# A ReLU-mean over rows: 127 rows a partition and a separate block of 128 rows, in place of 128 rows a partition

## The chip, the cores and the metric

The kernel runs on one core of a Trainium2 chip. The metric is device time in microseconds (us), measured outside the profile. An execution's span on the core is about 1.8 us shorter than its device time.

## The reference

```
x: 32 x 512 x 1024 float32          # 16,384 rows of 1024 values, 67.1 MB
out = mean(maximum(x, 0), axis=-1)  # 16,384 float32, 65.5 KB
```

There are few operations per byte: each value is read once and added once.

## The kernel before

Partition p holds rows 128p to 128p+127, so two neighbouring partitions start 512 KiB apart in memory. Seven tiles of 16 rows a partition are loaded in three rotating buffers. The last 16 rows are loaded in pieces of 8, 4, 2 and 1 rows, and the very last row in three column pieces. Rows go alternately to VectorE and ScalarE (L20 and L15 in the profile). Only SyncE's queue (SP) loads and stores.

```
def dve_row(nc, src, acc, init=None):                      # VectorE, L20
    nc.vector.tensor_scalar(out=src, in0=src, scalar1=0.0, scalar2=init,
        op0=ALU.max, op1=ALU.add, accum_out=acc)
# act_row (ScalarE, L15): activation Relu with accum_out=acc
...
xr = xf.rearrange("(p j) d -> p j d", p=P, j=J)            # J = 128
outr = out.flatten().rearrange("(p j) -> p j", p=P, j=J)
NB = 16; full = J // NB - 1
row_pieces = [8, 4, 2, 1]; col_pieces = [512, 256, 256]
...
for t in range(full):
    j0 = t * NB
    xt = in_pool.tile([P, NB, D], F32, name="xt")          # bufs=3
    nc.sync.dma_start(out=xt, in_=xr[:, j0:j0 + NB, :])
    rows(xt, 0, NB, j0)
...
for n in row_pieces:
    nc.sync.dma_start(out=xt[:, lo:lo + n, :], in_=xr[:, j0 + lo:j0 + lo + n, :])
    lo += n
# the last row's three column pieces are loaded here
...
for n in row_pieces[:-1]:
    rows(xt, lo, n, j0)
    lo += n
act_row(nc, prev[:, :512], part[:, 0:1])                   # row 126, one half each
dve_row(nc, prev[:, 512:], part[:, 1:2])
# row 127: 256 + 256, 128 + 128 columns side by side, then 256 on VectorE
...
nc.vector.scalar_tensor_tensor(out=res[:, J - 1:J], ...)
nc.sync.dma_start(out=outr, in_=res)                       # 512 B a partition
```

Of the kernel before, what the change touches and what calls it, by code (L numbers as in the profile page):

```python
# [1 line left out]

# [4 lines left out]

F32 = mybir.dt.float32
ALU = mybir.AluOpType
ACT = mybir.ActivationFunctionType  # L10


def act_row(nc, src, acc):

    nc.scalar.activation(out=src, in_=src, func=ACT.Relu, accum_out=acc)  # L15


def dve_row(nc, src, acc, init=None):

    nc.vector.tensor_scalar(  # L20
        out=src, in0=src, scalar1=0.0, scalar2=init,
        op0=ALU.max, op1=ALU.add, accum_out=acc,
    )


@with_exitstack
def kernel(
    ctx: ExitStack,
    tc: tile.TileContext,
    x: bass.AP,  # L30
    out: bass.AP,
):
    nc = tc.nc
    P = nc.NUM_PARTITIONS
    xf = x.flatten_outer_dims()
    R, D = xf.shape
    assert R % P == 0
    J = R // P
    inv = 1.0 / D
    xr = xf.rearrange("(p j) d -> p j d", p=P, j=J)  # L40
    outr = out.flatten().rearrange("(p j) -> p j", p=P, j=J)
    xlast = xr[:, J - 1, :]

    NB = 16
    full = J // NB - 1

    row_pieces = [8, 4, 2, 1]
    assert sum(row_pieces) == NB - 1
    col_pieces = [512, 256, 256]
    assert sum(col_pieces) == D  # L50

    in_pool = ctx.enter_context(tc.tile_pool(name="in", bufs=3))
    res_pool = ctx.enter_context(tc.tile_pool(name="res", bufs=1))
    sums = res_pool.tile([P, J], F32)
    res = res_pool.tile([P, J], F32)
    part = res_pool.tile([P, 10], F32)

    def rows(xt, lo, n, j0):

        for k in range(lo, lo + n):  # L60
            j = j0 + k
            (dve_row if j % 2 else act_row)(nc, xt[:, k, :], sums[:, j:j + 1])

    def finish(lo, hi):
        nc.gpsimd.tensor_scalar(  # L65
            out=res[:, lo:hi], in0=sums[:, lo:hi], scalar1=inv, scalar2=0.0, op0=ALU.mult, op1=ALU.add,
        )

    for t in range(full):
        j0 = t * NB  # L70
        xt = in_pool.tile([P, NB, D], F32, name="xt")
        nc.sync.dma_start(out=xt, in_=xr[:, j0:j0 + NB, :])  # L72
        rows(xt, 0, NB, j0)

    j0 = full * NB
    xt = in_pool.tile([P, NB, D], F32, name="xt")
    prev, last = xt[:, NB - 2, :], xt[:, NB - 1, :]
    lo = 0
    for n in row_pieces:
        nc.sync.dma_start(out=xt[:, lo:lo + n, :], in_=xr[:, j0 + lo:j0 + lo + n, :])  # L80
        lo += n
    c = 0
    for w in col_pieces:
        nc.sync.dma_start(out=last[:, c:c + w], in_=xlast[:, c:c + w])
        c += w

    finish(0, j0)
    lo = 0
    for n in row_pieces[:-1]:
        rows(xt, lo, n, j0)  # L90
        lo += n
    finish(j0, j0 + lo)



    act_row(nc, prev[:, :512], part[:, 0:1])
    dve_row(nc, prev[:, 512:], part[:, 1:2])
    nc.gpsimd.tensor_scalar(  # L98
        out=res[:, J - 2:J - 1], in0=part[:, 0:1], scalar1=part[:, 1:2], scalar2=inv, op0=ALU.add, op1=ALU.mult,
    )  # L100
    act_row(nc, last[:, :256], part[:, 2:3])
    dve_row(nc, last[:, 256:512], part[:, 3:4])
    nc.gpsimd.tensor_scalar(  # L103
        out=part[:, 4:5], in0=part[:, 2:3], scalar1=inv, scalar2=0.0, op0=ALU.mult, op1=ALU.add,
    )
    act_row(nc, last[:, 512:640], part[:, 5:6])
    dve_row(nc, last[:, 640:768], part[:, 6:7], init=part[:, 3:4])
    nc.scalar.activation(  # L108
        out=part[:, 7:8], in_=part[:, 5:6], func=ACT.Identity, scale=inv, bias=part[:, 4:5],
    )  # L110
    dve_row(nc, last[:, 768:], part[:, 8:9], init=part[:, 6:7])
    nc.vector.scalar_tensor_tensor(  # L112
        out=res[:, J - 1:J], in0=part[:, 8:9], scalar=inv, in1=part[:, 7:8], op0=ALU.mult, op1=ALU.add,
    )
    nc.sync.dma_start(out=outr, in_=res)


# [1 line left out]
_INS = ['x']  # L119
_OUTS = [((32, 512), 'float32')]  # L120


# [23 lines left out]
```

## Time and profile before

| | before |
|---|---|
| device time, median of 4 | 164.65 us |
| the profiled execution: device time, span | 164.37 us, 162.6 us |
| VectorE, ScalarE busy | 46%, 43% |
| first input packet starts, last one ends | 1.75 us, 158.65 us |
| VectorE's last result, issue of the store | 160.08 us, 160.15 us |

The packet times come from the trace's DMA records: each has a start, a duration and a size. They were put on the profile's axis by the first memset, which is at 0.24 us. I call the stretch from the last input packet's end to the end of VectorE's last result the *tail*: 1.43 us here.

The page of the kernel before gives the bound: the load queue's packets fill 96.2% of the 16 DMA engines' time, and the chain that ended last is made of input transfers.

```profile
DVE 74.8 (46%) x135; ACT 69.6 (43%) x134; POOL 1.2 (1%) x8
...
DMA packets 2162, 67.19 MB, mean 413 GB/s; under 512 B 240, under 2 KB 624, under 8 KB 880
...
q1 hardware_dynamic: 2160, 67.18, 96.2%
...
DMA 84%; DVE 13%; SPq 1%; issue 0%; DVEq 0%
...
out_dram<-res SPq DMA_DIRECT2D x1, 64.0 KB, 1.5
```

VectorE's 13% of the chain needs care: two of its stretches, 9.2 us each, stand between a landing and the next load's issue, and earlier loads keep the DMA engines busy meanwhile (the DMA row has no gap). Only the third stretch, after the stream, adds to the span.

That stretch is in VectorE's timeline. The columns are start, duration (us), engine, line, operation, output and input; an idle time and its releaser follow in brackets where there is one.

```profile
154.03 1.22 DVE L20 TENSOR_SCALAR_CACHE_REDUCE xt<-xt 128x1024 f32<-128x1024 f32 x1
...
155.18 1.22 DVE L20 TENSOR_SCALAR_CACHE_REDUCE xt<-xt 128x1024 f32<-128x1024 f32 x1
156.32 0.08 DVE L20 DVE_READ_ACCUMULATOR xt<-xt 128x1 f32 x1
156.53 1.22 DVE L20 TENSOR_SCALAR_CACHE_REDUCE xt<-xt 128x1024 f32<-128x1024 f32 x1
157.67 0.08 DVE L20 DVE_READ_ACCUMULATOR xt<-xt 128x1 f32 x1
157.83 0.69 DVE L20 TENSOR_SCALAR_CACHE_REDUCE xt<-xt 128x512 f32<-128x512 f32 x1
...
158.47 0.42 DVE L20 TENSOR_SCALAR_CACHE_REDUCE xt<-xt 128x256 f32<-128x256 f32 x1
...
159.92 0.16 DVE L112 SCALAR_TENSOR_TENSOR res<-part 128x1 f32<-128x1 f32 x1
```

VectorE starts the four-row piece at 154.03 and could take a new row at 156.32, before the two-row piece is there (156.53). It then keeps up with the landings: 157.83 is the landing of row 126.

### The profile page before, as it was taken

To read this page: it belongs to the slowest core of one execution; us is meant where nothing else is said; L and a number is where in the kernel's file an instruction comes from. 1 tells how busy PE (TensorE), PEld (TensorE's weight loads), DVE (VectorE), ACT (ScalarE), POOL (GpSimd) and SP (SyncE) were. 2 spreads that over 40 slices of the span, in tenths; PEclk is the share of its full clock that TensorE was granted. 3 is DMA by queue.
4 is the path that set the end of the run, shared out by engine and by line. 5 is a ranking of instruction groups with operands and counts; after the bars stand their busy time and mean duration, and the time that the engine had idled before them with its cause. 6 is when DMAs were issued, how large, how long until landed. Compare 5 with 4: busy or idle time off the path is not lost.

```text
span 162.6 us, 358 instructions
## 1 busy us (share of the span) xinstructions
DVE 74.8 (46%) x135; ACT 69.6 (43%) x134; POOL 1.2 (1%) x8
## 2 busy tenths in 40 slices
DVE  0000039900696008940099201990049800698993
ACT  3000039700694008920099002980049600696882
POOL 0000000000000000000000000000000000000001
DMA  7979989989988997997997998997998997998980
GB/s 258 516 322 451 516 355 419 516 371 403 516 387 387 516 435 339 516 435 339 516 484 326 484 484 355 451 500 339 451 500 355 435 516 306 451 435 379 415 334 17
DMA packets 2162, 67.19 MB, mean 413 GB/s; under 512 B 240, under 2 KB 624, under 8 KB 880
## 3 DMA queue, kind: packets, MB, share of 16 engines
q1 hardware_dynamic: 2160, 67.18, 96.2%
q14 instruction: 2, 0.02, 0.0%
HBM read 67.11 MB, written 0.07 MB: 413 GB/s over the span
## 4 chain that ended last, share of the span: by engine, by line
DMA 84%; DVE 13%; SPq 1%; issue 0%; DVEq 0%
DMA xt<-in_x_dram 84%; DVE xt L20 13%; SPq L80 1%; SPq L72 0%; DVE res L112 0%; DVEq L20 0%; DVEq L112 0%
## 5 line engine op out<-in xcount | busy, mean ns | idle before, releaser
L20 DVE TENSOR_SCALAR_CACHE_REDUCE xt<-xt 128x1024 f32<-128x1024 f32 (+1 forms) x65 | 73.7, 1195 | 85.1 <-DMA xt<-in_x_dram 84.8
L15 ACT ACTIVATE xt<-xt 128x1024 f32<-128x1024 f32 (+1 forms) x66 | 67.0, 1016 | 89.2 <-DMA xt<-in_x_dram 89.2
L15 ACT ACTIVATION_READ_ACCUMULATOR xt<-xt 128x1 f32 x66 | 12.3, 187 | 0.0
L20 DVE DVE_READ_ACCUMULATOR xt<-xt 128x1 f32 x65 | 5.4, 83 | 0.0
L65 POOL TENSOR_SCALAR res<-sums 128x112 f32<-128x112 f32 (+1 forms) x2 | 0.5, 252 | 157.2 <-DVE xt L20 157.2
L15 ACT ACT_TABLE_LOAD x1 | 1.3, 1283 | 0.7 <-PEq L130 0.7
L20 DVE TENSOR_SCALAR_CACHE_REDUCE xt<-xt,part 128x128 f32<-128x128 f32 (+1 forms) x2 | 0.8, 412 | 0.1
L108 ACT ACTIVATE part<-part 128x1 f32<-128x1 f32 x1 | 0.3, 294 | 0.1
L98 POOL TENSOR_SCALAR res<-part 128x1 f32<-128x1 f32 x1 | 0.3, 264 | 0.6 <-ACT xt L15 0.6
L112 DVE SCALAR_TENSOR_TENSOR res<-part 128x1 f32<-128x1 f32 x1 | 0.2, 159 | 0.1
L103 POOL TENSOR_SCALAR part<-part 128x1 f32<-128x1 f32 x1 | 0.2, 191 | 0.1
L20 DVE DVE_READ_ACCUMULATOR xt<-xt,part 128x1 f32 x2 | 0.2, 83 | 0.0
L130 POOL MEMSET const-bfloat16-1.0<- 128x1 bf16 x1 | 0.1, 101 | 0.0
L130 POOL MEMSET const-uint8-127<- 128x1 uint8 x1 | 0.1, 101 | 0.0
L130 POOL MEMSET const-float32-0.0<- 128x1 f32 x1 | 0.1, 98 | 0.2 <-issue 0.2
L130 POOL MEMSET const-float32-1.0<- 128x1 f32 x1 | 0.1, 98 | 0.0
## 6 DMA issues: line engine op xcount, KB each, us to landing
xt<-in_x_dram SPq DMA_DIRECT2D x1, 4096.0 KB, 39.0
xt<-in_x_dram SPq DMA_DIRECT2D x1, 2048.0 KB, 43.5
xt<-in_x_dram SPq DMA_DIRECT2D x1, 1024.0 KB, 45.5
xt<-in_x_dram SPq DMA_DIRECT2D x1, 512.0 KB, 46.4
xt<-in_x_dram SPq DMA_DIRECT2D x1, 256.0 KB, 46.5
xt<-in_x_dram SPq DMA_DIRECT2D x2, 128.0 KB, 42.7
xt<-in_x_dram SPq DMA_DIRECT2D x7, 49.0
out_dram<-res SPq DMA_DIRECT2D x1, 64.0 KB, 1.5
```

Source lines behind the costliest of these rows:

```text
L15: nc.scalar.activation(out=src, in_=src, func=ACT.Relu, accum_out=acc)
L20: nc.vector.tensor_scalar(out=src, in0=src, scalar1=0.0, scalar2=init, op0=ALU.max, op1=ALU.add, accum_out=acc,)
L65: nc.gpsimd.tensor_scalar(out=res[:, lo:hi], in0=sums[:, lo:hi], scalar1=inv, scalar2=0.0, op0=ALU.mult, op1=ALU.add,)
L80: nc.sync.dma_start(out=xt[:, lo:lo + n, :], in_=xr[:, j0 + lo:j0 + lo + n, :])
L98: nc.gpsimd.tensor_scalar(out=res[:, J - 2:J - 1], in0=part[:, 0:1], scalar1=part[:, 1:2], scalar2=inv, op0=ALU.add, op1=ALU.mult,)
L103: nc.gpsimd.tensor_scalar(out=part[:, 4:5], in0=part[:, 2:3], scalar1=inv, scalar2=0.0, op0=ALU.mult, op1=ALU.add,)
L108: nc.scalar.activation(out=part[:, 7:8], in_=part[:, 5:6], func=ACT.Identity, scale=inv, bias=part[:, 4:5],)
L112: nc.vector.scalar_tensor_tensor(out=res[:, J - 1:J], in0=part[:, 8:9], scalar=inv, in1=part[:, 7:8], op0=ALU.mult, op1=ALU.add,)
L130: nc = _bacc.Bacc("TRN2", target_bir_lowering=False, num_devices=1)
```

## The change

The first 128 rows are loaded one to a partition, as one contiguous block. All other rows lie 127 to a partition, so the pitch between partitions is 508 KiB, no longer a power of two. The means of the first rows stand in one column; VectorE turns them in 32x32 blocks and ScalarE's queue stores them early. The odd count changes the last pieces from 8, 4, 2, 1 to 8, 4, 1, 1 rows, still followed by the split last row, and the final store from 512 to 508 B a partition.

```diff
-    xr = xf.rearrange("(p j) d -> p j d", p=P, j=J)
-    outr = out.flatten().rearrange("(p j) -> p j", p=P, j=J)
...                                            # outf = out.flatten()
+    M = J - 1
+    xr = xf[P:, :].rearrange("(p j) d -> p j d", p=P, j=M)
+    outr = outf[P:].rearrange("(p j) -> p j", p=P, j=M)
+    xfirst = xf[:P, :]
+    outfirst = outf[:P].rearrange("(q i) -> q i", i=32)
...
-    row_pieces = [8, 4, 2, 1]
+    row_pieces = [8, 4, 1, 1]
...
+    nc.sync.dma_start(out=x0, in_=xfirst)
+    nc.vector.memset(mean0, 0.0)
+    dve_row(nc, x0, mean0[:, 0:1])
+    nc.vector.tensor_scalar_mul(out=mean0[:, 0:1], in0=mean0[:, 0:1], scalar1=inv)
+    nc.vector.transpose(turned0, mean0)
     for t in range(full):
...
+        if t == 2:
+            nc.scalar.dma_start(out=outfirst, in_=turned0[0:P:32, :])
...
-    for n in row_pieces[:-1]:
+    for n in row_pieces[:2]:
         rows(xt, lo, n, j0)
...
-    act_row(nc, prev[:, :512], part[:, 0:1])
-    dve_row(nc, prev[:, 512:], part[:, 1:2])
+    for k in range(2):
+        act_row(nc, xt[:, lo + k, :512], part[:, 2 * k:2 * k + 1])
+        dve_row(nc, xt[:, lo + k, 512:], part[:, 2 * k + 1:2 * k + 2])
...          # the split last row is as before
```

More of the change, by code (lines that the diff above doesn't have):

```diff
@@ L39 @@
     inv = 1.0 / D
-    xr = xf.rearrange("(p j) d -> p j d", p=P, j=J)
-    outr = out.flatten().rearrange("(p j) -> p j", p=P, j=J)
-    xlast = xr[:, J - 1, :]
+    outf = out.flatten()
+    M = J - 1
[3 more added lines that the diff above has]
+    outfirst = outf[:P].rearrange("(q i) -> q i", i=32)
+    xlast = xr[:, M - 1, :]
     NB = 16
-    full = J // NB - 1
-    row_pieces = [8, 4, 2, 1]
-    assert sum(row_pieces) == NB - 1
+    full = M // NB
+    row_pieces = [8, 4, 1, 1]
+    assert full * NB + sum(row_pieces) + 1 == M
     col_pieces = [512, 256, 256]
@@ L53 @@
     res_pool = ctx.enter_context(tc.tile_pool(name="res", bufs=1))
-    sums = res_pool.tile([P, J], F32)
-    res = res_pool.tile([P, J], F32)
-    part = res_pool.tile([P, 10], F32)
+    sums = res_pool.tile([P, M], F32)
+    res = res_pool.tile([P, M], F32)
+    part = res_pool.tile([P, 12], F32)
     def rows(xt, lo, n, j0):
@@ L67, in finish @@
         )
+    x0 = res_pool.tile([P, D], F32)
+    mean0 = res_pool.tile([P, 32], F32)
+    turned0 = res_pool.tile([P, 32], F32)
+    nc.sync.dma_start(out=x0, in_=xfirst)
[3 more added lines that the diff above has]
+    nc.vector.transpose(turned0, mean0)
     for t in range(full):
@@ L76 @@
     xt = in_pool.tile([P, NB, D], F32, name="xt")
-    prev, last = xt[:, NB - 2, :], xt[:, NB - 1, :]
+    last = xt[:, NB - 2, :]
     lo = 0
@@ L92 @@
     finish(j0, j0 + lo)
-    act_row(nc, prev[:, :512], part[:, 0:1])
-    dve_row(nc, prev[:, 512:], part[:, 1:2])
+    for k in range(2):
+        act_row(nc, xt[:, lo + k, :512], part[:, 2 * k:2 * k + 1])
+        dve_row(nc, xt[:, lo + k, 512:], part[:, 2 * k + 1:2 * k + 2])
+        nc.gpsimd.tensor_scalar(
+            out=res[:, j0 + lo + k:j0 + lo + k + 1], in0=part[:, 2 * k:2 * k + 1],
+            scalar1=part[:, 2 * k + 1:2 * k + 2], scalar2=inv, op0=ALU.add, op1=ALU.mult,
+        )
+    act_row(nc, last[:, :256], part[:, 4:5])
+    dve_row(nc, last[:, 256:512], part[:, 5:6])
     nc.gpsimd.tensor_scalar(
-        out=res[:, J - 2:J - 1], in0=part[:, 0:1], scalar1=part[:, 1:2], scalar2=inv, op0=ALU.add, op1=ALU.mult,
+        out=part[:, 6:7], in0=part[:, 4:5], scalar1=inv, scalar2=0.0, op0=ALU.mult, op1=ALU.add,
     )
-    act_row(nc, last[:, :256], part[:, 2:3])
-    dve_row(nc, last[:, 256:512], part[:, 3:4])
-    nc.gpsimd.tensor_scalar(
-        out=part[:, 4:5], in0=part[:, 2:3], scalar1=inv, scalar2=0.0, op0=ALU.mult, op1=ALU.add,
-    )
-    act_row(nc, last[:, 512:640], part[:, 5:6])
-    dve_row(nc, last[:, 640:768], part[:, 6:7], init=part[:, 3:4])
-    nc.scalar.activation(
-        out=part[:, 7:8], in_=part[:, 5:6], func=ACT.Identity, scale=inv, bias=part[:, 4:5],
-    )
-    dve_row(nc, last[:, 768:], part[:, 8:9], init=part[:, 6:7])
+    act_row(nc, last[:, 512:640], part[:, 7:8])
+    dve_row(nc, last[:, 640:768], part[:, 8:9], init=part[:, 5:6])
+    nc.scalar.activation(
+        out=part[:, 9:10], in_=part[:, 7:8], func=ACT.Identity, scale=inv, bias=part[:, 6:7],
+    )
+    dve_row(nc, last[:, 768:], part[:, 10:11], init=part[:, 8:9])
     nc.vector.scalar_tensor_tensor(
-        out=res[:, J - 1:J], in0=part[:, 8:9], scalar=inv, in1=part[:, 7:8], op0=ALU.mult, op1=ALU.add,
+        out=res[:, M - 1:M], in0=part[:, 10:11], scalar=inv, in1=part[:, 9:10], op0=ALU.mult, op1=ALU.add,
     )
```

## The prediction

> **What bounds the kernel now.** It is a stream of 67.11 MB into the core. The page gives queue 1 96.2% of the 16 DMA engines' time, against VectorE 46% and ScalarE 43%; in the chain of waits the input transfers are 84% of the span and the 13% of VectorE lies inside the stream except at the end. In the trace's DMA records the first data packet starts at about 2.0 us and the last input packet ends at about 158.9 us. The 896 packets of 64 KiB have a mean of 2433 ns, which is 431 GB/s over 16 engines. The rest of the span is the tail: row 126 is seen at 157.83, VectorE works without a break to 160.08 (timeline), the store is issued at 160.15 and lands 1.5 us later.
>
> **What the change removes.** The pitch between partitions falls from 512 KiB to 508 KiB. The Trainium skill, "DMA: Bandwidth & Descriptors", section "Latency and other measured facts", has slow copies at row pitches of large powers of two (207 GB/s at 512 KiB against 214 with a padded 4 MiB pitch). Here the 64 KiB packets show no such loss: the same page's fabric ceiling ("Where 436 GB/s comes from", 435 GB/s) is 1% above 431. At most about 1 us is to be had; I expect about 0.
>
> **What it adds, off the critical path.** One 512 KiB load, one 128x1024 reduce (1.22 us), a scale and a block transpose on VectorE, done before the first big tile lands at about 22 us; one 512 B store from ScalarE's queue early on. Both engines idle for over 84 us: no effect.
>
> **What it changes on the critical path.**
> 1. Stream: a 128x1024 load in 4 KiB packets takes the place of half of the two-row piece. 4 KiB packets take 162 ns, 8 KiB packets 320 (310 typical): 8 x 2 x 162 against 8 x 315 per engine is +0.07 us.
> 2. Compute tail: the last pieces are 8, 4, 1, 1 rows and the split last row, in place of 8, 4, 2, 1. The four-row piece now lands later, about 4.0 us before the stream's end in place of 5.2. Before, it was seen at 154.03 and VectorE was free at 156.40, before the next piece (156.52). Now: seen at about 155.3, VectorE free at about 157.7, then two half rows of 0.64 us each (before: one) to 159.0, then the sequence for the last row (158.47 to 160.08 before, 1.61 us): ready at about 160.6. That is +0.5 us.
> 3. Final store: 508 B a partition in place of 512, unaligned in memory. The skill's page (Specifications) has a read-modify-write below 512 B. Before, a 512 B packet took 27 ns, 8 to an engine. I estimate +0.25 us (0 to 0.8).
>
> Sum: +0.8 us, less perhaps 0.1 from the pitch: **165.4 us**, range 164.5 to 166.4. Chances: faster by over 2% 0.02, within 2% 0.94, slower by over 2% 0.04.
>
> **What would show it.** Pitch: mean of the 64 KiB packets still 2.42 to 2.44 us. Stream: last input packet ends at 158.7 to 159.3. Tail: the last result on VectorE ends at 160.4 to 160.8, the two half-row pairs back to back. Store: from issue to landing 1.5 to 2.3 us. First rows: over before 10 us.
>
> **What would make it wrong.** A 508 KiB pitch that makes 64 KiB packets slower or faster than 2.43 us (each 1% is 1.6 us); a gap at the start between the small load and the first tile; a skew between engines (about 1.2 us at the end before) that grows.

## The result, and the profile after

The changed kernel took 164.62 us (median of 4, 164.31 to 164.72) against 164.65 us. The ratio is 0.9996, with a 95% interval from 0.9978 to 1.0013: the same time. (A ratio is the mean time of one kernel's fast runs over that of the other's of the same rounds, so not quite the ratio of the medians.) Repeated in a later session (e11 below) it had 0.9985 (0.9970 to 0.9999). The forecast rise of 0.8 us (1.0046) is outside both intervals, though 164.62 lies just inside the stated range, at its lower end.

The page after shows the same bound, the first rows' work done early, and the store one notch longer to its landing:

```profile
DVE 75.7 (46%) x140; ACT 68.9 (42%) x134; POOL 1.4 (1%) x9
...
q1 hardware_dynamic: 2304, 67.17, 96.1%
...
DMA 83%; DVE 14%; SPq 1%; issue 1%; DVEq 0%
...
x<-in_x_dram SPq DMA_DIRECT2D x1, 512.0 KB, 3.5
...
out_dram<-res SPq DMA_DIRECT2D x1, 63.5 KB, 1.7
```

In the timeline of all engines after, the added work is over at about 8 us. The first big tile lands long after that, so none of it reaches the span:

```profile
5.81 0.21 DVE L82 STREAM_TRANSPOSE turned<-mean 128x32 f32<-128x32 f32 x1
6.05 1.10 ACTq L88 DMA_DIRECT2D out_dram<-turned  x1
7.18 1.28 ACT L15 ACT_TABLE_LOAD   x1 [7.18 <-issue]
23.66 1.22 DVE L20 TENSOR_SCALAR_CACHE_REDUCE xt<-xt 128x1024 f32<-128x1024 f32 x1 [17.65 <-DMA xt<-in_x_dram]
```

VectorE's timeline at the end after, to be held against the one before:

```profile
155.13 1.22 DVE L20 TENSOR_SCALAR_CACHE_REDUCE xt<-xt 128x1024 f32<-128x1024 f32 x1
...
156.27 1.21 DVE L20 TENSOR_SCALAR_CACHE_REDUCE xt<-xt 128x1024 f32<-128x1024 f32 x1
157.41 0.08 DVE L20 DVE_READ_ACCUMULATOR xt<-xt 128x1 f32 x1
157.41 0.68 DVE L20 TENSOR_SCALAR_CACHE_REDUCE xt<-xt 128x512 f32<-128x512 f32 x1
...
158.02 0.68 DVE L20 TENSOR_SCALAR_CACHE_REDUCE xt<-xt 128x512 f32<-128x512 f32 x1
...
158.62 0.41 DVE L20 TENSOR_SCALAR_CACHE_REDUCE xt<-xt 128x256 f32<-128x256 f32 x1
...
160.07 0.16 DVE L130 SCALAR_TENSOR_TENSOR res<-part 128x1 f32<-128x1 f32 x1
```

The shape is as predicted: the four-row piece lands 1.1 us later, and from there VectorE has no break. But the last result ends at 160.23 us, 0.15 later than before, where 160.6 was forecast. The parts, by the traces:

| | before | after |
|---|---|---|
| last input packet ends | 158.65 | 158.54 |
| VectorE's last result ends | 160.08 | 160.23 |
| tail (difference) | 1.43 | 1.70 (from unrounded times) |
| final store: issued, its packets | 160.15, 160.99 to 161.34 | 160.29, 161.14 to 161.49 |
| mean of one store packet | 26.9 ns (512 B) | 27.0 ns (508 B) |
| median of a 64 KiB packet | 2418 ns | 2418 ns |

So the tail grew by 0.27 us and the store by nothing that the packets show, and the stream ended 0.1 us earlier where 0.07 later was forecast. One trace each can't settle a tenth of a microsecond; the experiments have to. Here the two traces aren't even alike: the profiled execution after took 164.56 us, close to its median, and the one before took 164.37, 0.28 under its own. The table therefore makes the stream's gain look too small. In e2, e3 and e4 below, whose streams are close to that of the kernel before, the last input packet ends at 158.82, 158.67 and 158.93, in executions of 164.82, 164.32 and 164.73 us.

### The profile page after: what moved, and what is told of

The parts are those of the page before. It is cut to its first block, busy times and chain, and to the rows that moved or that the text cites. A ratio compares the mean times of both kernels' runs of the same rounds, so it can differ in the third digit from the quotient of the medians.

```text
span 162.8 us, 369 instructions
## 1 busy us (share of the span) xinstructions
DVE 75.7 (46%) x140; ACT 68.9 (42%) x134; POOL 1.4 (1%) x9
## 4 chain that ended last, share of the span: by engine, by line
DMA 83%; DVE 14%; SPq 1%; issue 1%; DVEq 0%
DMA xt<-in_x_dram 83%; DVE xt L20 14%; SPq L86 0%; SPq L78 0%; SPq L96 0%; DVE res L130 0%; DVEq L20 0%; DVEq L130 0%
## 5 line engine op out<-in xcount | busy, mean ns | idle before, releaser
L20 DVE TENSOR_SCALAR_CACHE_REDUCE xt<-xt 128x1024 f32<-128x1024 f32 (+2 forms) x65 | 72.9, 1186 | 80.0 <-DMA xt<-in_x_dram 79.9
L15 ACT ACTIVATE xt<-xt 128x1024 f32<-128x1024 f32 (+2 forms) x66 | 66.5, 1009 | 83.4 <-DMA xt<-in_x_dram 83.4
L20 DVE TENSOR_SCALAR_CACHE_REDUCE x<-x 128x1024 f32<-128x1024 f32 x1 | 1.2, 1220 | 3.5 <-DMA x<-in_x_dram 3.5
```

The costliest lines, as they stand in the source:

```text
L15: nc.scalar.activation(out=src, in_=src, func=ACT.Relu, accum_out=acc)
```

## The experiments

The theory after the first look: the new tail costs about 0.27 us; the store costs nothing; something in the stream (the small contiguous load of the first 128 rows, which I call the *block*, or the 508 KiB pitch) gives about as much back. The rival: the tail has slack and costs nothing in time. Every kernel below was timed beside the kernel before on one chip. Differences in us are differences of mean times to the kernel before of the same chip. Two measures from the DMA records are used besides: the end of the last input packet, and the *start loss*. The start loss is, for the first 8 us and averaged over the 16 DMA engines, the idle time plus what the packets took over the median of their size; it is 2.8 us before (2.20 idle, 0.62 slow packets) and 2.4 us after (2.08, 0.35).

### Tail, small load, store: e1 to e4

e1, the changed kernel with the old tail:

```diff
-    row_pieces = [8, 4, 1, 1]
+    row_pieces = [7, 4, 2, 1]
-    for n in row_pieces[:2]:
+    for n in row_pieces[:3]:
...  # and one row in halves, as before the change, in place of two
```

> The changed kernel with the old tail (pieces 7, 4, 2, 1 and the split last row; all else as changed). Theory A, the new tail costs about 0.26 us that a quicker start of the stream (0.1 us) and noise hide: VectorE's last result comes about 1.43 us after the last input packet's end (1.69 in the changed kernel), and the time is 0.2 to 0.3 us below the changed kernel's, about 164.35 us, ratio to before about 0.998. Theory B, the tail costs nothing: no change against the changed kernel, about 164.6 us, ratio 1.000.

e2, the kernel before with the new tail:

```diff
-    row_pieces = [8, 4, 2, 1]
+    row_pieces = [9, 4, 1, 1]
...  # the last two of these rows in halves, as after the change
```

> The kernel before (512 KiB pitch) with the new tail alone (pieces 9, 4, 1, 1 and the split last row). Theory A: the last result comes about 1.69 us after the last input packet's end in place of 1.43, and the time is 164.85 to 164.95 us, ratio about 1.0015. Theory B: 164.65 us, ratio 1.000. The recorded prediction's own figure was +0.5 us, 165.15 us, ratio 1.003.

e3, the kernel before with a small first load:

```diff
+        if t == 0:
+            nc.sync.dma_start(out=xt[:, :1, :], in_=xr[:, :1, :])
+            nc.sync.dma_start(out=xt[:, 1:, :], in_=xr[:, 1:NB, :])
```

> The kernel before with its first tile loaded as 1 row and then 15 rows, pitch 512 KiB. Before, the sum of the packets' times over their medians (mean per engine) was 0.82 us, nearly all in the first packets; in the changed kernel 0.73 us (0.43 in the 64 KiB packets, 0.28 in the 4 KiB ones). Theory C, small first packets take the slow start more cheaply: excess falls to 0.7 us or below, the last input packet ends about 0.1 us earlier, about 164.55 us. Theory D, the 512 KiB pitch makes the first packets slow: excess stays at 0.8 us or above and the time is 164.65 to 164.75 us (0.08 more for the small packets).

e4, the kernel before with the new stores:

```diff
+        if t == 2:
+            nc.scalar.dma_start(out=outf[:P].rearrange("(q i) -> q i", i=32), in_=zero[0:P:32, :])
-    nc.sync.dma_start(out=outr, in_=res)
+    nc.sync.dma_start(out=outf[P:].rearrange("(p j) -> p j", p=P, j=J - 1), in_=res[:, 1:J])
```

> The kernel before with the changed kernel's two stores (wrong values on purpose: 508 B a partition at the 508 B pitch, behind an early store of 128 zeros). Theory E, 508 B stores cost what 512 B ones do: packets of about 27 ns, 164.65 us within 0.1. Theory F, as predicted, a read-modify-write shows: issue to end of the span grows by about 0.25 us, 164.9 us, ratio 1.0015.

| | ratio to before (95%) | difference | last input packet | tail |
|---|---|---|---|---|
| e1 old tail, rest changed | 0.9990 (0.9969 to 1.0010) | -0.19 | 158.47 | 1.54 |
| e2 new tail alone | 1.0022 (1.0007 to 1.0037) | +0.32 | 158.82 | 1.71 |
| e3 small first load, 512 KiB | 0.9996 (0.9983 to 1.0010) | -0.09 | 158.67 | 1.43 |
| e4 new stores alone | 1.0004 (0.9992 to 1.0016) | +0.04 | 158.93 | 1.46 |

e2 is the clear one: put into the kernel before, the new tail costs +0.32 us in time and lengthens the tail in the trace from 1.43 to 1.71. The rival falls. The interval (0.1 to 0.6 us) also holds the 0.5 that was forecast; that the size is about 0.3 rests on the traces. VectorE's timeline of e2 has the same unbroken rows as the changed kernel's:

```profile
155.43 1.22 DVE L20 TENSOR_SCALAR_CACHE_REDUCE xt<-xt 128x1024 f32<-128x1024 f32 x1
...
157.71 0.68 DVE L20 TENSOR_SCALAR_CACHE_REDUCE xt<-xt 128x512 f32<-128x512 f32 x1
...
158.32 0.68 DVE L20 TENSOR_SCALAR_CACHE_REDUCE xt<-xt 128x512 f32<-128x512 f32 x1
...
158.93 0.41 DVE L20 TENSOR_SCALAR_CACHE_REDUCE xt<-xt 128x256 f32<-128x256 f32 x1
...
160.37 0.16 DVE L112 SCALAR_TENSOR_TENSOR res<-part 128x1 f32<-128x1 f32 x1
```

e4 gave the wrong values it was meant to give; its 508 B packets take 27.1 ns, and the issue and landing lines of its last store are those of the changed kernel. Its time is that of the kernel before, with an interval (-0.1 to +0.26 us) that just reaches the forecast 0.25. The traces speak against that figure: from the issue of the last store to the end of the span it is 2.44 us before, 2.50 in e4, and 2.39 to 2.59 in the other kernels with 508 B stores apart from e10 and e15. So no cost of the store was found; one of up to about 0.1 us can't be excluded. e3's start loss, 2.67 us, is a little under the 2.8 before; its time shows no clear gain. e1 is only in the expected direction, and its tail in this one trace (1.54) is between the two; e12 repeats it.

```profile
out_dram<-res SPq DMA_DIRECT2D x1, 63.5 KB, 1.7
out_dram<-zero ACTq DMA_DIRECT2D x1, 0.5 KB
```

(The DMA issues of e4: queue, count, size and us from issue to landing. The landing of 1.7 us beside 1.5 before is not seen as time.)

### Order of the loads, more work in the tail, shorter packets: e5 to e8

e5 moves the load and the work of the first 128 rows behind the first big tile:

```diff
-    nc.sync.dma_start(out=x0, in_=xfirst)      # and the four VectorE lines after it
     for t in range(full):
...
         rows(xt, 0, NB, j0)
+        if t == 0:
+            nc.sync.dma_start(out=x0, in_=xfirst)   # and the four lines
```

> The changed kernel with the 512 KiB load of the first 128 rows issued behind the first big tile, so that the stream starts with 64 KiB packets at the 508 KiB pitch. Theory C (small first packets are what makes the start cheaper): the first 64 KiB packet of each engine takes 3.0 to 3.3 us again, and the time is 164.65 to 164.75 us. Theory D (the pitch is): the first packets stay at 2.5 to 2.7 us and the time is that of the changed kernel or lower.

e6 puts one more row for each engine behind the last large piece:

```diff
-    row_pieces = [8, 4, 1, 1]
+    row_pieces = [6, 6, 1, 1]
```

> The changed kernel with pieces 6, 6, 1, 1 in place of 8, 4, 1, 1: one more row for each of VectorE and ScalarE behind the last large piece, which lands at the same time. If VectorE's work after that landing bounds the tail (theory A), the time grows by about one row, 1.14 us, to 165.7 us. If the tail has slack (theory B), by less than 0.5 us.

e7 (in the kernel before) and e8 (in the changed kernel) load each full tile in four pieces, so that packets are 16 KiB:

```diff
-        nc.sync.dma_start(out=xt, in_=xr[:, j0:j0 + NB, :])
+        for q in range(0, NB, 4):
+            nc.sync.dma_start(out=xt[:, q:q + 4, :], in_=xr[:, j0 + q:j0 + q + 4, :])
```

> The kernel before with each full tile loaded in four pieces of 4 rows, so 16 KiB packets at the 512 KiB pitch. In the tail a 16 KiB packet took 611 ns median at this pitch, and 611 at 508 KiB. If the pitch does not matter, the median stays at 611 ns and the time rises by the packets' overhead, (4 x 611 - 2418) x 56 per engine = 1.5 us, to about 166.1 us (up to 0.5 less if the small start is cheaper). If the pitch slows shorter packets, the median or the excess grows, by 3% (5 us) if it were as in the Trainium skill's table.

> The changed kernel with each full tile loaded in four pieces of 4 rows: 16 KiB packets at the 508 KiB pitch. If the pitch does not matter: as e7_16k_512 within 0.3 us, about 166.1 us. If it does: 2 to 5 us faster than e7_16k_512.

| | ratio to before (95%) | difference | last input packet | tail |
|---|---|---|---|---|
| e5 small load second | 0.9990 (0.9975 to 1.0005) | -0.14 | 158.62 | 1.70 |
| e6 pieces 6, 6, 1, 1 | 1.0037 (1.0022 to 1.0052) | +0.63 | 158.24 | 2.84 |
| e7 16 KiB packets, 512 KiB pitch | 1.0131 (1.0109 to 1.0154) | +2.20 | 161.16 | 1.44 |
| e8 16 KiB packets, 508 KiB pitch | 1.0078 (1.0063 to 1.0093) | +1.30 | 160.05 | 1.72 |

e6 confirms how the tail works. Its last large piece is used from 154.83, about when the changed kernel's is (155.13), and one more row an engine moves the half rows from 157.41 to 158.26. The tail grows by 1.14 us, one row. VectorE's timeline of e6:

```profile
154.83 1.22 DVE L20 TENSOR_SCALAR_CACHE_REDUCE xt<-xt 128x1024 f32<-128x1024 f32 x1 [1.87 <-DMA xt<-in_x_dram]
...
158.26 0.68 DVE L20 TENSOR_SCALAR_CACHE_REDUCE xt<-xt 128x512 f32<-128x512 f32 x1
...
160.92 0.16 DVE L130 SCALAR_TENSOR_TENSOR res<-part 128x1 f32<-128x1 f32 x1
```

The time is only in part as expected: 165.44 us where 165.7 was forecast. It is 0.63 us over before, and not 1.4 (the growth of its tail over 1.43). So e6's stream would have gained 0.78 us, twice what the other kernels below show. Its stream does end early (158.24), but why by so much is not known.

e5 speaks against the small load *at the start* as the source of that gain. With 64 KiB packets first, the first packets were slow again (the slowest sixteen took 2.8 to 4.1 us, against a median of 2418 ns), as theory C said; yet the time is 0.14 us *under* before although e5 has the costlier tail (the interval is -0.4 to +0.1). Theory C's time of 164.65 to 164.75 fits in absolute numbers only because that chip's kernel before was at 164.79.

e7 against e8 shows the pitch plainly, for shorter packets. The median 16 KiB packet is 612 and 613 ns, but between 8 and 64 us the packets of e7 took 0.99 us per engine more than the median, those of e8 0.02 (one trace each; the block, which only e8 has, is over before 8 us). In the time e8 is 0.9 us below e7, and it would be about 1.2 with equal tails (1.44 and 1.72). Of this 0.3 may be the start (start loss 2.70 and 2.36), so that about 0.8 to 1.2 is the pitch's. That is less than the 2 to 5 us allowed for in the expectation, and far less than 3%.

### What made the stream end earlier: e9 to e15

e9 leaves the 512 KiB pitch and adds a contiguous first load, a repeat of rows 0 to 127:

```diff
+    nc.sync.dma_start(out=x0, in_=xf[:P, :])
+    dve_row(nc, x0, spare)
     for t in range(full):
```

> The kernel before plus an extra first load of rows 0 to 127, one to a partition (contiguous in memory; a repeat of 0.52 MB that only a spare reduce uses). Call start loss the idle time of the 16 DMA engines plus their first packets' excess over the median, both before 8 us and per engine: 2.8 to 2.9 us in the three runs with 64 KiB packets first at the 512 KiB pitch, 2.7 in e3 (4 KiB rows first at the 512 KiB pitch) and in e5 (64 KiB packets first at 508 KiB), 2.36 to 2.43 in the four runs that start with the contiguous small load. Theory G, that contiguous small load makes the start cheaper whatever pitch follows: start loss about 2.4 us, and the time grows by the load's 8 x 160 ns = 1.3 us less 0.4, to about 165.5 us. Theory H, the 508 KiB pitch behind it is needed: start loss 2.7 to 2.9 us, about 165.9 us.

e10 is e5 with the first tile split as in e3, so that the strided small load is the first traffic:

```diff
     for t in range(full):
...
-        nc.sync.dma_start(out=xt, in_=xr[:, j0:j0 + NB, :])
+        if t == 0:
+            nc.sync.dma_start(out=xt[:, :1, :], in_=xr[:, :1, :])
+            nc.sync.dma_start(out=xt[:, 1:, :], in_=xr[:, 1:NB, :])
+        else:
+            nc.sync.dma_start(out=xt, in_=xr[:, j0:j0 + NB, :])
```

> The changed kernel with its first big tile split into 1 and 15 rows and loaded first, and the load of the first 128 rows behind it: the stream starts with 4 KiB packets at the 508 KiB pitch. Theory G: start loss about 2.7 us as in e3, stream's end about 158.7 us, time about 0.2 us above the changed kernel. Theory H (small and 508 KiB): start loss about 2.4 us and the changed kernel's time plus 0.08 for the extra 4 KiB packets.

e11 is the changed kernel and e12 is e1, again, on one chip, with no edit:

> The changed kernel again, beside e12 on one chip, for the size of the two parts. If the start gains 0.4 us, the small packets cost 0.07 and the tail costs 0.27, the sum is -0.05 us, ratio to before 0.9997 (0.999 to 1.000). The recorded prediction was 1.0046.

> The changed kernel with the old tail (7, 4, 2, 1) again, for an interval with e1's: the gain of the start without the tail's cost, -0.3 us against before, ratio 0.998, and 0.2 to 0.3 us under e11. If it isn't below e11, the tail's cost does not reach the time.

e13 is e5 with e1's tail: of the change, the pitch, and the block in second place (and the stores, for which no cost was found). The label's "alone" says too much. Against the changed kernel:

```diff
-    row_pieces = [8, 4, 1, 1]
+    row_pieces = [7, 4, 2, 1]                       # and one row in halves, as in e1
-    nc.sync.dma_start(out=x0, in_=xfirst)           # and its work
...
+        if t == 0:
+            nc.sync.dma_start(out=x0, in_=xfirst)   # and its work, as in e5
```

> The 508 KiB pitch alone: the changed kernel with the old tail (7, 4, 2, 1) and with the load of the first 128 rows behind the first big tile. Theory P, the pitch brings the stream's gain: last input packet ends at about 158.4 us, time about 0.3 us under before (ratio 0.998), like e12. Theory S, the small contiguous load at the start does: stream's end at 158.7 to 158.8 us, time within 0.1 of before plus 0.07 (ratio 1.000).

e14 is the kernel before with a still smaller contiguous load:

```diff
+    x0 = res_pool.tile([P, 256], F32)
+    nc.sync.dma_start(out=x0, in_=xf[:32, :].rearrange("r (q c) -> (r q) c", c=256))
+    dve_row(nc, x0, spare)
```

> The kernel before (512 KiB pitch, 64 KiB packets) with an extra first load of the first 32 rows as 128 contiguous runs of 1 KiB (0.13 MB, a repeat that only a spare reduce uses). It costs 8 packets of 47 ns per engine, 0.38 us. Theory S: that is paid back by the cheaper start, time within 0.1 us of before (ratio 1.000). Theory P: +0.3 to +0.4 us (ratio 1.002).

e15 is the changed kernel with its first big tile split as in e3 (the edit shown for e10, in the changed kernel itself), behind the small contiguous load:

> The changed kernel with its first big tile loaded as 1 and 15 rows behind the contiguous small load. If e10's extra 1.4 us came from 4 KiB packets at the 508 KiB pitch as the first traffic: about the changed kernel's time, +0.1 us (about 164.6). If it came from the splitting itself (15-row packets, one more load in the queue): about 165.9 us again, and from issue of the last store to the end of the span 3.1 us as in e10, in place of 2.5.

| | ratio to before (95%) | difference | last input packet | tail | start loss |
|---|---|---|---|---|---|
| e9 extra contiguous load, 512 KiB | 1.0048 (1.0031 to 1.0065) | +0.78 | 159.70 | 1.46 | 2.69 |
| e10 small strided first, 508 KiB | 1.0075 (1.0061 to 1.0090) | +1.25 | 159.43 | 1.73 | 2.87 |
| e11 changed kernel again | 0.9985 (0.9970 to 0.9999) | -0.25 | 158.34 | 1.71 | 2.42 |
| e12 old tail, rest changed, again | 0.9973 (0.9958 to 0.9987) | -0.44 | 158.32 | 1.47 | 2.46 |
| e13 pitch, block second | 0.9986 (0.9972 to 1.0000) | -0.29 | 158.57 | 1.45 | 2.71 |
| e14 extra 32 rows, 512 KiB | 1.0032 (1.0018 to 1.0045) | +0.49 | 159.42 | 1.42 | 3.02 |
| e15 first tile split | 1.0074 (1.0047 to 1.0102) | +1.19 | 159.69 | 1.70 | 2.70 |

e12 against e11 is the tail in the time once more: 0.19 us. e13 is the new layout in the time, without the new tail: -0.29 us, with an interval that just touches 1. (Its stream ends at 158.57 us, between the 158.4 expected by theory P and the 158.7 of theory S.) Put beside the other runs at the 508 KiB pitch that load each full tile in one piece, e6 (-0.78) left aside, and less 0.27 us for the new tail where they have it, there are six readings of the stream's gain:

| | small contiguous load first | difference | less the tail's 0.27 |
|---|---|---|---|
| changed kernel | yes | -0.07 | -0.34 |
| e11 | yes | -0.25 | -0.52 |
| e1 | yes | -0.19 | -0.19 (old tail) |
| e12 | yes | -0.44 | -0.44 (old tail) |
| e5 | no | -0.14 | -0.41 |
| e13 | no | -0.29 | -0.29 (old tail) |

The mean is -0.37 us with the small load first and -0.35 without. The three kernels that have the 512 KiB pitch, all the bytes once and the same tail or one accounted for have +0.05 (e2 less 0.27), -0.09 (e3) and +0.04 (e4). So the gain goes with the new layout, and having the small load *first* adds nothing that the time shows, though each reading is uncertain by about 0.25 us. But pitch and block are not separated: every one of the six loads the block, first or second, and the 512 KiB kernels e2, e3 and e4 do not. The one 512 KiB kernel that loads the block whole, e9, took 0.5 us less than its extra packets account for (below). So a rival stands: the block gives the gain, wherever it is loaded. It could be tested by e9 with its extra load second, or by the 508 KiB pitch without the block. The start loss tells a different story from the time: it falls from 2.8 to 2.7 in e5 and e13 (as in e3, at 512 KiB) and to 2.4 only with the small load first as well (not in e15, where the next tile is split: 2.7). What the engines win in the first 8 us with the small load, about 0.3 us, is not found again in the time.

Two more expectations failed. In e14 the small load was too small: its packets were done at 2.1 us (median) while the next load's first packets started at 2.30 to 3.81 us, so the engines stood idle. It measured a gap, and says nothing on theory S. e9 grew by only 0.78 us for 1.28 us of packets (8 of 160 ns), as theory G has it, though its start loss is what theory H has. Its interval (0.5 to 1.1 us) excludes the full 1.28 us, and so speaks for the block and against the pitch as the only source; with theory H's start loss the contradiction stays open.

e10 and e15 cost 1.2 us. For e10 at most 0.2 more than the changed kernel was expected; for e15 this was one of two outcomes laid down. e15 (four executions, 165.31 to 166.37 us, the slowest of them profiled) shows that it is the splitting of the first tile at the 508 KiB pitch and not the order of loads. In the DMA records the engines end unequally (the records don't name the engine; the packets fit into 16 chains with overlaps of a few ns, so I count 64 KiB packets that end within one packet's 2.4 us as those of different engines): in e15 the last 64 KiB packets of the three latest engines end at 141.19, 141.00 and 140.33 us, and the sixth latest at 139.31. Before, the latest was at 138.93 and the sixth at 138.53. That lag is then carried to the end of the stream, and the final store also takes longer to land in both:

```profile
out_dram<-res SPq DMA_DIRECT2D x1, 63.5 KB, 2.3
```

(That is e15's DMA issue of the final store; before it was 1.5 us.) Why splitting did this at 508 KiB and not at 512 KiB (e3, -0.09 us) is not known.

The version that beats both kernels is e1/e12: the 127-row layout with pieces 7, 4, 2, 1. It measured 164.30 and 164.19 us (medians). The second interval lies clear of 1, the first does not; the gain is about 0.2% and less than the 2% that would be called faster. Its timeline at the end (e12) shows VectorE waiting for landings again, as in the kernel before, and not running behind them:

```profile
153.74 1.22 DVE L20 TENSOR_SCALAR_CACHE_REDUCE xt<-xt 128x1024 f32<-128x1024 f32 x1 [0.66 <-DMA xt<-in_x_dram]
...
156.24 1.22 DVE L20 TENSOR_SCALAR_CACHE_REDUCE xt<-xt 128x1024 f32<-128x1024 f32 x1
...
157.38 0.08 DVE L20 DVE_READ_ACCUMULATOR xt<-xt 128x1 f32 x1
157.52 0.69 DVE L20 TENSOR_SCALAR_CACHE_REDUCE xt<-xt 128x512 f32<-128x512 f32 x1
...
159.63 0.16 DVE L127 SCALAR_TENSOR_TENSOR res<-part 128x1 f32<-128x1 f32 x1
```

## Why the prediction was right or wrong

The class (within 2%) was right, which with a 0.94 chance given to it says little, and so was the bound. The direction and the sum were wrong: +0.8 us forecast, about 0 measured (-0.07 and -0.25 us in two sessions). The sum failed in three terms, all of them too slow: stream +0.07 against about -0.35, tail +0.5 against about +0.27, store +0.25 against about 0. That no change is measured is in part luck: a gain of the stream that was not foreseen pays for the tail.

1. **Stream, "+0.07 us" and pitch "about 0".** Measured: about -0.35 us for the new layout, pitch and block together (partly read from the runs that it explains; e13 alone has -0.29). This is the largest of the three failed terms, about half of the miss. The reasoning was that 64 KiB packets already ran at 431 GB/s, 1% under the 435 GB/s ceiling in the Trainium skill ("DMA: Bandwidth & Descriptors", "Where 436 GB/s comes from"), so that "at most about 1 us is to be had". The bound was right and the guess of 0 inside it was not. The check that the prediction named, the mean of the 64 KiB packets, stayed within its range (2425.6 ns) and the median did not move at all (2418 ns). The traces put the gain mostly into idle time of the DMA engines, at the start and at the end of the stream: counted from the start of the span to the end of the stream, it is 2.6 to 2.7 us per engine in the traces of before, e2 and e4 and 2.2 to 2.3 in those of e1, e5, e11, e12 and e13. Some traces do not fit a split by pitch: at 512 KiB e3 has 2.4 and e9, with the block, 2.15, and the changed kernel's own trace has 2.5. About 0.1 us, in the first 8 us of e5 and e13 (start loss 2.7 against 2.8), is the pitch's, since their block comes later. For the rest it is not shown whether pitch or block brings it. The cost of the extra 4 KiB packets (0.07 us) can't be told from the noise.

2. **Tail, "+0.5 us".** The mechanism was right and its size was not: +0.27 us in the traces (1.43 to 1.70), +0.32 and +0.19 us in time (e2; e11 over e12). Step by step: the four-row piece was used at 155.13, not 155.3 (the stream ended earlier); its two rows took 2.28 us, not 2.4; the two half rows took 1.21, not 1.3; the last sequence took 1.61, as forecast. The second and third come from one slip: the end of a READ_ACCUMULATOR was taken for the moment VectorE is free, where the next row starts together with it (1.14 us a row, 0.60 a half row), and one interval before the change (157.83 to 158.47) had been set by a landing (ScalarE starts at 158.47 too).

3. **Store, "+0.25 us".** The step that failed is the cost of a read-modify-write. Measured: 27.0 ns a packet for 508 B and 26.9 for 512 B, and +0.04 us (e4, -0.1 to +0.26). The Trainium skill, "DMA: Bandwidth & Descriptors", section "Specifications", has a read-modify-write below 512 B; nothing of it shows here, at 128 packets of 508 B.

4. **First rows and early store off the critical path:** right. They are over at about 8 us, and VectorE next waits 17.65 us for the first tile.

5. **Packet times.** The packet times in the prediction (2.0 and 158.9 us) were put on the profile's axis 0.24 us too late; against the memset they are 1.75 and 158.65. The landings were read from the timeline, so the tail's estimate moved little by it (3.91 us from the four-row piece to the stream's end, where 4.0 was used).

The skill's row-pitch table ("Latency and other measured facts" of the same page) was weighed and put aside. It has 207 GB/s at 512 KiB against 214 with a padded 4 MiB pitch, 3%, for 16 KiB rows. Here 16 KiB packets gained 0.8 to 1.2 us of 167, at most 0.7%, from 512 to 508 KiB, and the new layout with 64 KiB packets about 0.35 us, 0.2%, which may be the block's. The direction of the page's number held; its size did not carry over.

## What to carry to other kernels

When a stream is at its ceiling, what is left is at its ends, and the tail is a queue. Work out from the starts of rows, not from the ends of their records, when each engine is free and which piece has landed by then. By an estimate from these traces, give each last piece at most about twice the rows of the next (here a row lands in about 1.2 us, and the two engines together reduce one in 0.57; 7, 4, 2, 1 kept up, 8, 4, 1, 1 ran 0.27 us behind, 6, 6, 1, 1 ran 1.4 us behind). A term that is "about zero" because the mean of the large packets looks ideal is still uncertain by the few tenths of a microsecond that the first packets and the slowest of 16 engines make; put them in the range. Changes of 0.2% need the parts measured in opposite kernels (a part taken out here, put in there), since one timing with ±0.25 us can't show them. And compare the device time of a profiled execution with the median of its kernel before reading tenths of a microsecond from its trace.

## What the Trainium skill lacked or had wrong

- "DMA: Bandwidth & Descriptors", "Specifications": below 512 B the engine is said to read, modify and write. Stores of 508 B at a 508 B pitch took 27.0 ns a packet against 26.9 ns for 512 B, and no measurable time (e4: +0.04 us, -0.1 to +0.26). No cost of a few bytes under the limit was found here.
- The same page, "Latency and other measured facts", row pitch: the table is of copies between HBM tensors with 16 KiB rows. For loads into the core, 508 KiB in place of 512 KiB was worth at most 0.7% with 16 KiB packets (e7, e8) and at most about 0.2% with 64 KiB packets, at an unchanged median packet. What the 16 KiB packets lost to the pitch lay before 64 us (0.99 us per engine between 8 and 64 us at 512 KiB, 0.02 at 508 KiB).
- I found no statement on that page that the first packets of a stream are slower. At the 512 KiB pitch 13 first packets of 64 KiB took 3.0 to 3.3 us where the median is 2.42, which is most of the 0.62 us of slow packets per engine; at 508 KiB (e5) the slowest sixteen took 2.8 to 4.1 us.
- Nor how large a lag between the engines a load can leave: the page's "The descriptor swizzle" gives each engine its partitions, and in e15 the latest engine was 1.9 us behind the sixth latest at 141 us, and the stream then ended 1.2 us later than the changed kernel's (159.69 against 158.54).
